# A latent-attention preparation on Trainium2: rotation, root, tables and constants put in another order and on another engine

## The chip, the cores and the metric

The kernel runs on one core of one Trainium2 chip. The metric is device time in microseconds, the median of several executions. The engines of a core are TensorE (PE in the profile, its weight loads PEld), VectorE (DVE), ScalarE (ACT), GpSimd (POOL) and SyncE (SP), whose queue issues nearly all transfers here. Each engine takes its instructions in the order in which they were compiled, and waits on semaphores where an input or a buffer is not there yet.

## The reference, cut to what matters

One layer of a decoder with three attention branches over 2048 tokens of width 1024: `x + W_out(concat(A, B, C) * silu(z))`. Branch A, multi-head latent attention with 8 heads, is the one whose preparation is changed:

```
q  = (rms_norm(cq, q_norm_g) @ w_uq).reshape(b, s, 8, 96)
kv = (rms_norm(ckv, kv_norm_g) @ w_ukv).reshape(b, s, 8, 128)
k_nope, v = kv[..., :64], kv[..., 64:]
k = concatenate([k_nope, broadcast(k_rope)], -1)
q = rms_norm(q, qn_g);  k = rms_norm(k, kn_g)
q = concatenate([q[..., :64], rope(q[..., 64:], pos)], -1)      # the same for k
o = softmax(causal(q k^T / sqrt(96))) v
```

Branch B is differential attention (4 heads with two softmax maps each, an RMS norm on its output), branch C attention into 256 memory tokens.

## The kernel before

**Stages.** The program is one list of steps, each for one block of 512 tokens (b = 0 to 3) and one group of heads: four steps `m` (memory), eight `d` (differential), sixteen `a` (latent: groups g = 0 to 3 of two heads). A step is prepared (`prep_m`, `prep_d`, `prep_a`), then its attention maps run (`Map`: scores into the PSUM tile `st`, an Exp on ScalarE at L506, the low part `plo` of the result on VectorE at L507, the products with V into `pv`), then a post stage (`post_d`, `post_y`) gates and transposes its output. Other work (projections, gates, output projection) is fed in between as generators.

**Order.** A loop at the end of `hybrid_block` picks at each turn the preparation, the fill or the map whose due position comes first, and each piece gets a priority. Nothing of this is the final order: the tile framework (`TileContext(nc, schedule_with_timeline_sim=True)`) then gives every engine its order with a timeline simulated at compile time, taking at each moment what is ready and has the best priority. So an instruction can be placed far ahead of where its line stands, when its inputs and its buffer are free, and every changed line can move others.

**One latent preparation, `prep_a`.** TensorE projects four tiles of 128 tokens; ScalarE copies queries `q` (L844) and keys `kn` (L845) out of PSUM and makes V. ScalarE squares the keys (L853) and the queries (L855); VectorE sums the squares (L854, L857). GpSimd makes the step's rotary tables times the norm weights (`rope_tabs`, four multiplies, L332 to L335, into the tile `rtab`, which has one buffer), adds the shared key part's squares (L861), and takes the inverse root in `rstd_of`: an addition of eps at L97 and a power of -0.5 at L101. With the root, GpSimd scales the shared rotated key (L866); VectorE scales the keys' 64 own columns (L871), multiplies them with the norm weights `g_n` (L872), and scales the queries (L874). GpSimd has rotated the queries' last 32 columns in place (`rope_in_place`, five instructions, L354 to L358, the first two by the sine into a scratch that is part of the squares' tile). The rotation doesn't need the root, and the root doesn't need the rotation; L874 needs both.

For each of the two heads the result is then split into a high and a low f16 part in a stack tile (`ks` for K, `qs` for Q; all stacks of the kernel share six buffers): ScalarE copies the high part (L880, L886), VectorE subtracts for the low part (L881, L887), GpSimd fills columns 96 to 127 with a constant (memsets at L879 and L885, 128 x 256 f16 each), and SP issues a transposing transfer into `kT` or `qB`. A stack buffer becomes free when its transposing transfer has read it. `est_block` then computes rough score maxima (L398, tiles `pe`, `ec`, `er`) and writes them into column 96 of `qs`.

**`post_d`.** The differential output's norm: eight squares on ScalarE (L596), `rstd_of` (L97, L101), then one more GpSimd multiply by 1/64 (L599) ahead of VectorE's L602.

The functions that the diff touches, and what calls them:

Of the kernel before, what the change touches and what calls it, by code (L numbers as in the profile page):

```python
# [15 lines left out]
AF = mybir.ActivationFunctionType  # L16
ALU = mybir.AluOpType
# [8 lines left out]
EPS = 1e-6  # L26
NEG = -1.0e30
WS = 64.0
MS = 32.0
# [11 lines left out]
def hybrid_block(ctx: ExitStack, tc: tile.TileContext, x, mem, positions, norm_g, w_in, mla_q_norm_g,  # L41
# [46 lines left out]
    gx = gain_cols(norm_g, NK, "gx", WS)  # L88
    gm = gain_cols(mem_norm_g, NK, "gm", WS, G)

    def rstd_of(ss, shape, name, tag="rstd"):
        r = sm.tile([P, 32 if tag == "rstd" else 8], F32, tag=tag, name=name)
        n = int(np.prod(shape))
        rv = r[:, 0:n]
        if len(shape) == 2:
            rv = rv.rearrange("p (a b) -> p a b", b=shape[1])
        G.tensor_scalar(rv, ss, EPS, None, ALU.add)  # L97
        m = mhalf
        if len(shape) == 2:
            m = m.unsqueeze(2)  # L100
        G.tensor_tensor(rv, rv, m.broadcast_to([P] + list(shape)), ALU.pow)  # L101
        return rv
# [96 lines left out]
    def new_qkv(name):  # L199
        return wk.tile([P, 4, 256], F32, tag="qkv", name=name, bufs=2)  # L200
# [103 lines left out]
    g_q = gain_row(mla_qn_g, 96, "g_q")  # L304
# [21 lines left out]
    def rope_tabs(b, g, name):  # L326

        tb = wk.tile([P, 2, 4, 32], F32, tag="rtab", name=f"rt_{name}", bufs=1)
        c = cos_t[:, 4 * b:4 * b + 4, :]
        s = sin_t[:, 4 * b:4 * b + 4, :]  # L330
        g1, g2 = _bc(g[:, 0:16], 1, 4), _bc(g[:, 16:32], 1, 4)
        G.tensor_tensor(tb[:, 0, :, 0:16], c, g1, ALU.mult)  # L332
        G.tensor_tensor(tb[:, 0, :, 16:32], c, g2, ALU.mult)
        G.tensor_tensor(tb[:, 1, :, 0:16], s, g2, ALU.mult)
        G.tensor_tensor(tb[:, 1, :, 16:32], s, g1, ALU.mult)  # L335
        return tb
# [12 lines left out]
    def rope_in_place(q, tb, nh, eng, tmp):  # L349

        tmp = tmp.rearrange("p (t h d) -> p t h d", t=4, d=32)
        C = _bc(tb[:, 0], 2, nh)
        Sn = _bc(tb[:, 1], 2, nh)
        eng.tensor_tensor(tmp[..., 0:16], q[..., 16:32], Sn[..., 0:16], ALU.mult)  # L354
        eng.tensor_tensor(tmp[..., 16:32], q[..., 0:16], Sn[..., 16:32], ALU.mult)
        eng.tensor_tensor(q, q, C, ALU.mult)
        eng.tensor_tensor(q[..., 0:16], q[..., 0:16], tmp[..., 0:16], ALU.subtract)
        eng.tensor_tensor(q[..., 16:32], q[..., 16:32], tmp[..., 16:32], ALU.add)  # L358
# [231 lines left out]
    def post_d(st, y):  # L590
        y8 = y.rearrange("p t h d -> p (t h) d")
        ss = sm.tile([P, 8], F32, tag="yss", name=f"yss_{st.name}")
        ys = new_ys(4 + st.g, st.b)
        sink = ys[:, 0].rearrange("p t k -> p (t k)")
        for i in range(8):
            A.activation(sink[:, 64 * i:64 * i + 64], y8[:, i, :], AF.Square, scale=1.0 / 8.0, accum_out=ss[:, i:i + 1])  # L596
        yield 1.0
        r = rstd_of(ss[:, 0:8], [8], f"yr_{st.name}", "rstd_y")
        G.tensor_scalar(r, r, 1.0 / WS, None, ALU.mult)  # L599
        yield 1.0  # L600
        yield 1.0
        V.tensor_tensor(y8, y8, _bc(r, 2, 64), ALU.mult)  # L602
        yield 1.0
        yf = y.rearrange("p t h d -> p t (h d)")
        V.tensor_tensor(yf, yf, st.z, ALU.mult)
        yield 1.0
        yield from finish(st, yf, 4 + st.g, ys)
# [216 lines left out]

    def prep_a(st):
        g, b, nm = st.g, st.b, st.name
        q = new_qkv(f"qkv_{nm}")[:, :, 0:192].rearrange("p t (h d) -> p t h d", d=96)
        knt = tmp4(f"kn_{nm}")
        kn = knt[:, 0:768].rearrange("p (t h d) -> p t h d", t=4, d=96)
        vt = new_v(b, nm)  # L830
        G.memset(vt[:, :, :, 64:65], WS)
        for t in range(4):
            ps = ps_p.tile([P, 512], F32, tag="pp", name="pp")
            q0, k0 = 192 * g, 256 * g
            first = True
            for c in range(2):
                for hx, hw in ((0, 0), (0, 1), (1, 0)):
                    T.matmul(ps[:, 0:192], lhsT=lat_q[b][:, t, hx, c, :], rhs=wuq[c][:, hw, q0:q0 + 192], start=first,
                             stop=False, skip_group_check=True)
                    first = False  # L840
            for i, (hx, hw) in enumerate(((0, 0), (0, 1), (1, 0))):
                T.matmul(ps[:, 192:448], lhsT=lat_kv[b // 2][:, b % 2, t, hx, :], rhs=wukv[0][:, hw, k0:k0 + 256],
                         start=False, stop=(i == 2), skip_group_check=True)
            A.activation(q[:, t], ps[:, 0:192].rearrange("p (h d) -> p h d", d=96), AF.Copy, scale=1.0 / WS)  # L844
            A.activation(kn[:, t, :, 0:64], ps[:, 192:320].rearrange("p (h d) -> p h d", d=64), AF.Copy, scale=1.0 / WS)  # L845
            put_v(vt[:, t], ps[:, 320:448].rearrange("p (h d) -> p h d", d=64))
            yield 1.6
        sqt = tmp4(f"sqq_{nm}")
        sq = sqt[:, 0:768].rearrange("p (t h d) -> p t h d", t=4, d=96)
        ss = sm.tile([P, 2, 8], F32, tag="ssa", name=f"ss_{nm}")  # L850
        for i, m in enumerate((sqt, knt)):
            sk = m[:, 768:1024].rearrange("p (t h d) -> p t h d", t=2, d=64)
            A.activation(sk, kn[:, 2 * i:2 * i + 2, :, 0:64], AF.Square, scale=1.0 / math.sqrt(96))  # L853
            V.reduce_sum(ss[:, 1, 4 * i:4 * i + 4], sk.rearrange("p t h d -> p (t h) d"), axis=AX.X)  # L854
        A.activation(sq, q, AF.Square, scale=1.0 / math.sqrt(96))  # L855
        yield 1.0
        V.reduce_sum(ss[:, 0, :], sq.rearrange("p t h d -> p (t h) d"), axis=AX.X)  # L857
        tb = rope_tabs(b, g_q[:, 64:96], nm)
        yield 1.0
        s4 = ss[:, 1, :].rearrange("p (t h) -> p t h", h=2)  # L860
        G.tensor_tensor(s4, s4, _bc(ss_kr[b], 2, 2), ALU.add)  # L861
        r = rstd_of(ss.rearrange("p a b -> p (a b)"), [16], f"r_{nm}")
        rq = r[:, 0:8].rearrange("p (t h) -> p t h", h=2)
        rk = r[:, 8:16].rearrange("p (t h) -> p t h", h=2)
        yield 1.0
        G.tensor_tensor(kn[..., 64:96], _bc(krot[b], 2, 2), _bc(rk, 3, 32), ALU.mult)  # L866
        rope_in_place(q[..., 64:96], tb, 2, G, sqt[:, 768:1024])
        yield 1.0
        yield 1.0
        yield 1.0  # L870
        V.tensor_tensor(kn[..., 0:64], kn[..., 0:64], _bc(rk, 3, 64), ALU.mult)  # L871
        V.tensor_tensor(kn[..., 0:64], kn[..., 0:64], _bc(_bc(g_n, 1, 2), 1, 4), ALU.mult)  # L872
        yield 1.0
        V.tensor_tensor(q, q, _bc(rq, 3, 96), ALU.mult)  # L874
        kT = bigt([P, 2, 4, 2, P], f"kT_{nm}") if b in AB else kvp.tile([P, 2, 4, 2, P], F16, tag="kT", name=f"kT_{nm}")
        st.qs, st.qB = [], []
        for h in range(2):
            ks = stack([P, 4, 2, P], f"ks{h}_{nm}")
            G.memset(ks[:, :, :, 96:128], MS)  # L879
            A.activation(ks[:, :, 0, 0:96], kn[:, :, h], AF.Copy)  # L880
            V.tensor_tensor(ks[:, :, 1, 0:96], kn[:, :, h], ks[:, :, 0, 0:96], ALU.subtract)  # L881
            SP.dma_start_transpose(kT[:, h].rearrange("p t l k -> p (t l) k"), ks.rearrange("p t l d -> p (t l d)"))
            yield 1.0
            qs = stack([P, 2, 4, P], f"qs{h}_{nm}")
            G.memset(qs[:, :, :, 96:128], 0.0)  # L885
            A.activation(qs[:, 0, :, 0:96], q[:, :, h], AF.Copy)  # L886
            V.tensor_tensor(qs[:, 1, :, 0:96], q[:, :, h], qs[:, 0, :, 0:96], ALU.subtract)  # L887
            st.qs.append(qs)
            st.qB.append(new_qb([P, 2, 4, P], f"qB{h}_{nm}"))
            SP.dma_start_transpose(st.qB[h].rearrange("p l t k -> p (l t) k"), qs.rearrange("p l t d -> p (l t d)"))  # L890
            yield 1.0
        st.kTs = st.prev.kTs + [kT] if b else [kT]
        st.Vs = st.prev.Vs + [vt] if b else [vt]
        yield 1.0
        yield 1.0
        for h in range(2):
            yield from est_block(st, h, 1, lambda m: st.qs[h][:, 0, :, 96], lambda m, t: st.qB[h][0:96, 0, t, :],
                                 lambda m, c, n: st.kTs[c][0:96, h, 0:n, 0, :])
            SP.dma_start_transpose(st.qB[h][:, 0], st.qs[h][:, 0].rearrange("p t d -> p (t d)"))
            ready.add((nm, h))  # L900
            yield 1.0
# [361 lines left out]
```

## Time and profile before

| | us |
|---|---|
| runs shown: median (lowest to highest) of three | 1380.5 (1380.03 to 1385.78) |
| the profiled execution, its own time | 1382.39 |
| its span, first to last instruction | 1380.7 |
| mean granted TensorE clock | 0.983 |
| TensorE busy, with weight loads apart | 1297.6 |
| VectorE busy | 1113.6 |
| ScalarE busy | 902.8 |
| GpSimd busy | 353.4 |

A row of waits or idle time says who waited and which instruction released it; `L` numbers are lines of the kernel. A matmul counts as busy while it is in the pipeline, so a busy TensorE is not always one at its peak, and the granted clock is a share of full speed.

### The profile page before, as it was taken

To read this page: it belongs to the slowest core of one execution; us is meant where nothing else is said; L and a number is where in the kernel's file an instruction comes from. 1 tells how busy PE (TensorE), PEld (TensorE's weight loads), DVE (VectorE), ACT (ScalarE), POOL (GpSimd) and SP (SyncE) were. 2 spreads that over 40 slices of the span, in tenths; PEclk is the share of its full clock that TensorE was granted. 3 is DMA by queue.
4 is the path that set the end of the run, shared out by engine and by line. 5 is a ranking of instruction groups with operands and counts; after the bars stand their busy time and mean duration, and the time that the engine had idled before them with its cause. 6 is when DMAs were issued, how large, how long until landed. Compare 5 with 4: busy or idle time off the path is not lost.

```text
span 1380.7 us, 35076 instructions
## 1 busy us (share of the span) xinstructions
PE 1297.6 (94%) x13616; PEld 834.4 (60%) x13616; DVE 1113.6 (81%) x2649; ACT 902.8 (65%) x2163; POOL 353.4 (26%) x549
## 2 busy tenths in 40 slices
PE   5988999999999999999999999999998988999998
PEld 2443556667677767767776656656665665655554
DVE  4657888879888867888998888988898888986745
ACT  6656544687877646786986567766766777774521
POOL 2322132403052233113212233232353333200000
PEclk9999999999999999999999999999999999999999
DMA  7998844323113322447345275446535443275452
GB/s 229 199 210 179 183 109 98 59 59 87 42 24 71 78 38 56 78 115 190 118 98 142 55 147 146 104 93 157 117 70 123 124 96 64 43 149 157 138 192 69
DMA packets 294263, 155.53 MB, mean 113 GB/s; under 512 B 239952, under 2 KB 272848, under 8 KB 294096
## 3 DMA queue, kind: packets, MB, share of 16 engines
q1 hardware_dynamic: 294064, 153.29, 47.1%
q8 instruction: 106, 1.74, 0.5%
q14 instruction: 61, 0.50, 0.1%
q0 software_dynamic: 32, 0.00, 0.0%
HBM read 61.75 MB, written 34.34 MB: 70 GB/s over the span
## 4 chain that ended last, share of the span: by engine, by line
PE 53%; DVE 14%; DMA 10%; POOL 9%; ACT 8%; issue 5%; SPq 1%; ACTq 0%; POOLq 0%; DVEq 0%
PE pp L187 6%; PE pp L188 6%; PE pp L189 6%; PE pe L398 5%; DVE plo L507 4%; PE pv L518 3%; PE pv L516 3%; PE pv L536 3%; PE st L572 3%; PE pp L957 3%; PE pp L958 3%; PE pp L959 3%; POOL r_a L101 2%; PE st L916 2%; PE st L917 2%
## 5 line engine op out<-in xcount | busy, mean ns | idle before, releaser
L506 ACT ACTIVATE p<-st 128x512 f32<-128x512 f32 (+3 forms) x672 | 356.1, 550 | 178.0 <-PE st L918 72.2
L507 DVE TENSOR_TENSOR plo<-p 128x512 f16<-128x512 f32 (+3 forms) x672 | 405.6, 615 | 61.9 <-ACT p L506 58.7
L407 ACT ACTIVATE ec<-pe 128x512 bf16<-128x512 f32 (+3 forms) x384 | 197.6, 536 | 34.1 <-PE pe L400 15.2
L516 PEld LDWEIGHTS <-p 128*128 128x128 bf16 x2304 | 187.0, 99 | 49.3 <-issue 5.1
L518 PEld LDWEIGHTS <-p 128*128 128x128 bf16 x2304 | 173.8, 98 | 41.5 <-issue 4.4
L408 DVE TENSOR_TENSOR er<-er,ec 128x512 bf16<-128x512 bf16 (+3 forms) x384 | 141.0, 377 | 29.9 <-ACT ec L407 15.1
L404 ACT ACTIVATE er<-pe 128x512 bf16<-128x512 f32 x192 | 110.2, 606 | 44.2 <-DVE mx_d L413 14.1
L536 PEld LDWEIGHTS <-plo 128*128 128x128 f16 x2304 | 123.6, 98 | 24.0 <-DVE plo L507 8.6
L916 PE MATMUL st<-qB_a,kT_a 97*128 97x512 f16 (+1 forms) x320 | 112.6, 352 | 19.2 <-ACT p L506 14.3
L189 PEld LDWEIGHTS <-ht_x 128*128 128x128 f16 x896 | 87.8, 98 | 54.8 <-ACT ht_x L137 5.1
L188 PEld LDWEIGHTS <-ht_x 128*128 128x128 f16 x896 | 87.8, 98 | 50.2 <-issue 6.4
L572 PE MATMUL st<-qB_d,kT_d 97*128 97x512 f16 (+1 forms) x320 | 112.2, 355 | 6.0 <-DMA qB_d<-s_d 2.9
L516 PE MATMUL pv<-V_d,p 128*128 128x65 f16 x1088 | 116.4, 194 | 0.8 <-DVE y_d L579 0.8
L187 PEld LDWEIGHTS <-ht_x 128*128 128x128 f16 x896 | 87.8, 98 | 46.6 <-issue 2.9
L518 PE MATMUL pv<-V_d,p 128*128 128x64 f16 x1088 | 115.9, 196 | 0.0
L516 PE MATMUL pv<-V_a,p 128*128 128x65 f16 x1088 | 113.9, 194 | 0.4 <-DVE y_a L923 0.4
L518 PE MATMUL pv<-V_a,p 128*128 128x64 f16 x1088 | 113.2, 196 | 0.0
L917 PE MATMUL st<-qB_a,kT_a 96*128 96x512 f16 (+1 forms) x320 | 112.3, 351 | 0.0
L398 PE MATMUL pe<-kT_d,qB_d 96*128 96x512 f16 (+2 forms) x320 | 106.4, 351 | 6.0 <-ACT ec L407 3.5
L918 PE MATMUL st<-qB_a,kT_a 96*128 96x512 f16 (+1 forms) x320 | 111.6, 349 | 0.0
L398 PE MATMUL pe<-kT_a,qB_a 96*128 96x512 f16 (+2 forms) x320 | 102.4, 353 | 6.6 <-DMA qB_a<-qs_a 3.1
L189 PE MATMUL pp<-w_d,ht_x 128*128 128x512 f16 x256 | 97.0, 379 | 0.0
(294 smaller groups left out, 3356.1 us busy)
## 6 DMA issues: line engine op xcount, KB each, us to landing
xt_x<-in_x_dram SPq DMA_DIRECT2D x16, 512.0 KB, 4.6
xr<-in_x_dram SPq DMA_DIRECT2D x16, 512.0 KB, 3.7
part<-xr SPq DMA_DIRECT2D x16, 512.0 KB, 3.1
ysc<-yt SPq DMA_DIRECT2D x31, 256.0 KB, 2.1
yl<-ysc SPq DMA_DIRECT2D x15, 512.0 KB, 4.4
zsc<-zc SPq DMA_DIRECT2D x48, 128.0 KB, 2.2
xa<-part SPq DMA_DIRECT2D x12, 512.0 KB, 3.6
out_dram<-xa SPq DMA_DIRECT2D x12, 512.0 KB, 3.3
```

Source lines behind the costliest of these rows:

```text
L187: T.matmul(ps[:, :n], lhsT=ht[:, 0, k], rhs=wt[:, 0, :n], start=(k == 0), stop=False)
L188: T.matmul(ps[:, :n], lhsT=ht[:, 0, k], rhs=wt[:, 1, :n], start=False, stop=False)
L189: T.matmul(ps[:, :n], lhsT=ht[:, 1, k], rhs=wt[:, 0, :n], start=False, stop=(k == NK - 1))
L398: T.matmul(ps[:, 0:n], lhsT=lhs(m, t), rhs=rhs(m, c, n // P), start=True, stop=c < b)
L407: A.activation(ec[:, 0:n], ps[:, 0:n], AF.Copy)
L408: V.tensor_tensor(er[:, t % 2, 0:n], er[:, t % 2, 0:n], ec[:, 0:n], ALU.max)
L506: A.activation(p32[:, :n], ps[:, :n], AF.Exp, scale=self.scale)
L507: V.tensor_tensor(plo[:, :n], p32[:, :n], phi[:, :n], ALU.subtract)
L516: T.matmul(pvv[:, t, 0:65], lhsT=phi[:, c], rhs=vt[:, 0:65], start=(j == 0 and t == 0), stop=False, skip_group_check=True)
L518: T.matmul(pvv[:, t, 0:64], lhsT=phi[:, c], rhs=vt[:, 65:129], start=False, stop=False, skip_group_check=True)
L536: last["pv"] = T.matmul(pvv[:, t, 0:65], lhsT=plo[:, c], rhs=vt[:, 0:65], start=False, stop=(j == self.njt - 1), skip_group_check=True)
L572: T.matmul(ps[:, :n], lhsT=st.kTs[j // 4][0:97, h, j % 4, m % 2, :], rhs=st.qB[h][0:97, t0:4, m % 2, :], start=True, stop=not diag)
```

## The change

Four things change in `prep_a`, one in `post_d`. (1) `rope_tabs` is called at the top of `prep_a`. (2) `rope_in_place` is issued ahead of L861 and the root, in place of behind L866. (3) The multiply by the norm weights `g_n` is issued ahead of the root, on keys that aren't scaled yet. (4) The four memsets of a step go from GpSimd to VectorE, each behind the subtract into the same tile (`tc.issue_after` puts an instruction behind a given one on its engine). (5) `post_d` folds the factor 1/64 into the squares' scale and eps, by a new argument of `rstd_of`, and drops L599.

```
-    def rstd_of(ss, shape, name, tag="rstd"):
+    def rstd_of(ss, shape, name, tag="rstd", eps=EPS):
...
-        G.tensor_scalar(rv, ss, EPS, None, ALU.add)
+        G.tensor_scalar(rv, ss, eps, None, ALU.add)
...
     def post_d(st, y):
...
-            A.activation(sink[:, 64 * i:64 * i + 64], y8[:, i, :], AF.Square, scale=1.0 / 8.0, accum_out=ss[:, i:i + 1])
-        yield 1.0
-        r = rstd_of(ss[:, 0:8], [8], f"yr_{st.name}", "rstd_y")
-        G.tensor_scalar(r, r, 1.0 / WS, None, ALU.mult)
+            A.activation(sink[:, 64 * i:64 * i + 64], y8[:, i, :], AF.Square, scale=WS / 8.0, accum_out=ss[:, i:i + 1])
+        yield 1.0
+        r = rstd_of(ss[:, 0:8], [8], f"yr_{st.name}", "rstd_y", EPS * WS * WS)
...
     def prep_a(st):
         g, b, nm = st.g, st.b, st.name
+        tb = rope_tabs(b, g_q[:, 64:96], nm)
...
         V.reduce_sum(ss[:, 0, :], sq.rearrange("p t h d -> p (t h) d"), axis=AX.X)
-        tb = rope_tabs(b, g_q[:, 64:96], nm)
-        yield 1.0
+        V.tensor_tensor(kn[..., 0:64], kn[..., 0:64], _bc(_bc(g_n, 1, 2), 1, 4), ALU.mult)
+        yield 1.0
+        rope_in_place(q[..., 64:96], tb, 2, G, sqt[:, 768:1024])
         s4 = ss[:, 1, :].rearrange("p (t h) -> p t h", h=2)
         G.tensor_tensor(s4, s4, _bc(ss_kr[b], 2, 2), ALU.add)
         r = rstd_of(ss.rearrange("p a b -> p (a b)"), [16], f"r_{nm}")
...
         G.tensor_tensor(kn[..., 64:96], _bc(krot[b], 2, 2), _bc(rk, 3, 32), ALU.mult)
-        rope_in_place(q[..., 64:96], tb, 2, G, sqt[:, 768:1024])
...
         V.tensor_tensor(kn[..., 0:64], kn[..., 0:64], _bc(rk, 3, 64), ALU.mult)
-        V.tensor_tensor(kn[..., 0:64], kn[..., 0:64], _bc(_bc(g_n, 1, 2), 1, 4), ALU.mult)
...
         for h in range(2):
             ks = stack([P, 4, 2, P], f"ks{h}_{nm}")
-            G.memset(ks[:, :, :, 96:128], MS)
             A.activation(ks[:, :, 0, 0:96], kn[:, :, h], AF.Copy)
-            V.tensor_tensor(ks[:, :, 1, 0:96], kn[:, :, h], ks[:, :, 0, 0:96], ALU.subtract)
+            lo = V.tensor_tensor(ks[:, :, 1, 0:96], kn[:, :, h], ks[:, :, 0, 0:96], ALU.subtract)
+            with tc.issue_after(lo.ins):
+                V.memset(ks[:, :, :, 96:128], MS)
...
             qs = stack([P, 2, 4, P], f"qs{h}_{nm}")
-            G.memset(qs[:, :, :, 96:128], 0.0)
             A.activation(qs[:, 0, :, 0:96], q[:, :, h], AF.Copy)
-            V.tensor_tensor(qs[:, 1, :, 0:96], q[:, :, h], qs[:, 0, :, 0:96], ALU.subtract)
+            lo = V.tensor_tensor(qs[:, 1, :, 0:96], q[:, :, h], qs[:, 0, :, 0:96], ALU.subtract)
+            with tc.issue_after(lo.ins):
+                V.memset(qs[:, :, :, 96:128], 0.0)
```

## Rows read from the trace of the kernel before

**Rows 1.** The page's busy time: us (share of the span) xinstructions.
```profile
PE 1297.6 (94%) x13616; PEld 834.4 (60%) x13616; DVE 1113.6 (81%) x2649; ACT 902.8 (65%) x2163; POOL 353.4 (26%) x549
```

**Rows 2.** Busy time by stretch; behind the engines: granted clock, DMA share, GB/s.
```profile
680.00:1250.00 570.00, 534.46 (x6126) 352.65 (x6124) 499.75 (x1191) 401.41 (x983) 175.76 (x285) 0.97 0.48 108
...
700.00:750.00 50.00, 48.92 (x583) 33.86 (x581) 47.94 (x118) 38.55 (x96) 13.04 (x23) 1.00 0.49 125
```

**Rows 3.** Waits: engine and line, what released it, total us, times, longest.
```profile
POOL qs_a L885 <- DMA kT_a<-ks_a: 59.3, 12, 11.3
...
ACT qs_a L886 <- DVE qkv_a L874: 17.7, 7, 6.7
...
DVE kn_a L871 <- POOL r_a L101: 16.2, 10, 4.3
...
PE st L916 <- ACT p L506: 14.3, 14, 4.3
```

**Rows 4.** Timeline of 1046 to 1062 us: start, us, engine, line [idle before].
```profile
1046.41 0.92 ACT L855 ACTIVATE sqq_a<-qkv_a 128x768 f32<-128x768 f32 x1
...
1048.77 0.31 POOL L885 MEMSET qs_a<- 128x256 f16 x1 [0.45 <-DMA kT_a<-ks_a]
1049.05 2.20 POOL L354 TENSOR_TENSOR sqq_a<-qkv_a,rt_a 128x128 f32<-128x128 f32 x1
...
1053.44 0.32 POOL L332 TENSOR_TENSOR rt_a<-cos_t,g_q 128x64 f32<-128x64 f32 x1
...
1055.70 2.92 POOL L101 TENSOR_TENSOR r_a<-r_a,mhalf 128x16 f32<-128x16 f32 x1
...
1061.78 0.37 PE L916 MATMUL st<-qB_a,kT_a 97*128 97x256 f16 x1 [4.34 <-ACT p L506]
```

**Rows 5.** Timeline of 1006 to 1021 us.
```profile
1006.22 0.88 ACT L855 ACTIVATE sqq_a<-qkv_a 128x768 f32<-128x768 f32 x1
...
1008.66 0.31 POOL L879 MEMSET ks_a<- 128x256 f16 x1 [1.56 <-DMA qB_a<-qs_a]
...
1020.24 0.38 PE L398 MATMUL pe<-kT_a,qB_a 96*128 96x512 f16 x1 [1.94 <-ACT ec L407]
```

**Rows 6.** Timeline of 1101 to 1111 us.
```profile
1101.73 0.86 ACT L855 ACTIVATE sqq_a<-qkv_a 128x768 f32<-128x768 f32 x1
...
1104.20 0.31 POOL L885 MEMSET qs_a<- 128x256 f16 x1 [4.76 <-DVE ss_a L857]
...
1105.82 0.96 POOL L354 TENSOR_TENSOR sqq_a<-qkv_a,rt_a 128x128 f32<-128x128 f32 x1
...
1109.77 0.28 ACT L845 ACTIVATE kn_a<-pp 128x128 f32<-128x128 f32 x1 [2.70 <-POOL qkv_a L358]
...
1110.92 0.48 PE L916 MATMUL st<-qB_a,kT_a 97*128 97x384 f16 x1 [3.49 <-ACT p L506]
```

**Rows 7.** Busy time in three stretches of 10 us, columns as in Rows 2.
```profile
1020.00:1030.00 10.00, 9.75 (x95) 6.66 (x95) 10.00 (x24) 7.83 (x22) 3.92 (x10) 0.83 0.28 54
1060.00:1070.00 10.00, 8.22 (x84) 6.46 (x84) 9.76 (x21) 8.06 (x23) 0.39 (x2) 0.83 0.62 145
1110.00:1120.00 10.00, 9.08 (x109) 7.24 (x109) 8.52 (x18) 6.64 (x19) 5.24 (x6) 0.69 0.26 57
```

**Rows 8.** The chain that ended last, by engine, share of the span.
```profile
PE 53%; DVE 14%; DMA 10%; POOL 9%; ACT 8%; issue 5%; SPq 1%; ACTq 0%; POOLq 0%; DVEq 0%
```

**Rows 9.** Groups by line and form: xcount | busy us, mean ns | idle before.
```profile
L507 DVE TENSOR_TENSOR plo<-p 128x256 f16<-128x256 f32 x64 | 27.1, 423 | 6.8 <-ACT p L506 6.6
...
L408 DVE TENSOR_TENSOR er<-er,ec 128x256 bf16<-128x256 bf16 x48 | 14.6, 303 | 2.9 <-ACT ec L407 1.4 <-ACT er L404 1.0
...
L872 DVE TENSOR_TENSOR kn_a<-kn_a,g_n 128x512 f32<-128x512 f32 x16 | 11.0, 685 | 0.0
...
L421 DVE TENSOR_SCALAR qs_a<-mx_a 128x4 f16<-128x4 f32 x32 | 5.7, 177 | 0.4
...
L599 POOL TENSOR_SCALAR yr_d<-yr_d 128x8 f32<-128x8 f32 x8 | 2.0, 252 | 0.7
```

## The prediction

> **What bounds the kernel now.** I read the page's busy shares first, then busy time by stretch, then the list of waits, then the timeline around single waits. TensorE is busy 1297.6 of 1380.7 us [rows 1], so whatever the change does on other engines, it can give back only what TensorE idles or runs at the lower clock: 83.1 us idle in the span. `prep_a`, which holds most of the diff, runs 16 times, nearly all of it in 680 to 1250 us. There TensorE is busy 534.46 of 570 us at a granted clock of 0.97 [rows 2]: 35.5 us idle, and 0.03 x 570 = 17 us of full-speed time lost to the clock. These 52 us are all that the main part of the change can win. In the same stretch VectorE is busy 499.75 of 570 us, 88%: it is the second bound, and it is given more work here.
>
> The waits tell where TensorE's idle time comes from [rows 3]. TensorE waits 14.3 us for the score buffer `st`, which ScalarE's Exp (L506) frees; ScalarE stands 17.7 us before L886 until VectorE has scaled the queries (L874); VectorE stands 16.2 us before L871 until GpSimd has the root (L101). Each engine takes its instructions in order, so a late root stops VectorE, then ScalarE, then TensorE. And GpSimd stands a further 59.3 us before L885, a memset, until an earlier transposing transfer has freed the stack buffer it fills. Most of that is harmless, GpSimd being busy only 353.4 us. It costs where the next step's rotation is queued behind it.
>
> Three places show that, and they hold the largest of TensorE's waits that go back to this chain:
> - 1057 us [rows 4]: ScalarE has the squares (L855) at 1046.41 + 0.92 = 1047.33, but the L885 memset waits for a transfer until 1048.77. Only then do the rotation (L354, 1049.05), the next step's tables (L332, 1053.44) and the root (L101, 1055.70, 2.92 us) follow. TensorE idles 4.34 us.
> - 1018 us [rows 5]: the L879 memset stands in the middle of the rotation until 1008.66 + 0.31; the squares were there at 1007.10. TensorE idles 1.94 us.
> - 1107 us [rows 6]: the memset at 1104.20 comes ahead of L354 at 1105.82, though the squares were there at 1102.59. The rotation's end (L358) is what ScalarE's L845 waits for (2.70 us, its buffer is the rotation's scratch), and TensorE idles 3.49 us.
> Behind each, the granted clock falls: 0.83, 0.83 and 0.69 in the 10 us after or around it [rows 7], a mixture of the two levels 2.4 and 1.2 GHz. That costs 1.7 + 1.7 + 3.1 = 6.5 us.
>
> **Constants by VectorE: GpSimd's side.** 64 memsets (two tiles, two heads, 16 steps) leave GpSimd's queue, and with them their waits. In the first place the rotation's multiplies by the sine need only the queries, and the third multiply could start with the squares at 1047.33; it started after L354's end at 1051.25, 3.9 us later. In the second it went on at 1008.97 and could have at 1007.10, 1.9 us. In the third L354 could start with the end of the squares at 1102.59, if VectorE's sums free its scratch by then, in place of 1105.82: 3.2 us. TensorE's gaps are each a little larger than these, so they shrink by the whole: 3.9 + 1.9 + 3.2 = 9.0 us. Bounds: nothing (another late instruction takes the memset's place) to 9.8 us, the three gaps. I take 9.0, because in each place the rows lead from the memset to the gap without another wait. Of the clock's 6.5 us I take half, 3.2; bounds 0 and 6.5. Next late after the memset is ScalarE's copy into the same stack buffer, which waits for the same transfer as before; nothing there gets worse.
>
> **Constants by VectorE: VectorE's side.** No VectorE memset is in this trace. Bounds from rows [rows 9]: above the smallest f16 write of VectorE, 0.177 us (L421), and below a two-operand f32 instruction over 256 columns, 0.423 (L507); I take 0.303 (L408, 256 16-bit columns), which it is nearest to. 64 x 0.303 = 19.4 us more VectorE work. The memset waits for nothing new: the subtract ahead of it has already written the tile. Behind it on VectorE are the low parts `plo`; on SP the transposing transfer now starts a memset later. What VectorE time costs at the end I price by its share of the chain that ended last, 14%, and the transfers by theirs, 10% [rows 8]: 19.4 x 0.24 = 4.6 us. Bounds: 64 x 0.177 x 0.14 = 1.6 us, and, with VectorE never free, 64 x 0.423 x 0.88 = 23.8 us. I take 4.6, as VectorE has 12% free time on average.
> The Trainium skill (VectorE: DVE Perf Modes, section "Zero memsets can be issued as uint32 (trn2)") says that a memset takes one cycle per element whatever the type; at the 0.96 GHz of its table my estimate from it is 256 / 0.96 = 267 ns, 17.1 us in all, which would make the term 4.1 in place of 4.6. No run here shows it yet; it speaks against any hope that the moved memsets are nearly free.
>
> **Norm weights ahead of the root.** L872 (16 x 0.685 = 11.0 us [rows 9]) leaves the stretch between root and K's copies for VectorE's wait before the root. At 14% that is a gain of 1.5 us; bounds nothing, and 10 x 0.685 = 6.9 us if it fills each of the ten waits. I take 1.5.
> The Trainium skill (SBUF — State Buffer, section "Who interferes with whom") says that a VectorE instruction with two SBUF inputs contends with a GpSimd one that reads SBUF, and L872, such a one, moves beside the rotation. The trace has L354 at 0.96 us [rows 6] and at 2.20 [rows 4], which may be this; my estimate is 11.0 us at GpSimd's 9%, a loss of 1.0 us. I leave it out, since VectorE runs other instructions with two operands there anyway.
>
> **Tables first, rotation first.** In 13 of the 16 steps the trace already has the rotation ahead of the root, and between them the tables of the *next* step: from L332 to the root 1053.44 to 1055.70, 2.3 us with two small instructions of the root's own among them [rows 4]. The order is the scheduler's: the table tile has one buffer, which becomes free when L356 has read it, and GpSimd is given whatever is ready. The diff moves where the tables are issued, not when the buffer becomes free, so I expect them to stay in front of the root: 0. Bound: 13 x 2.3 = 30 us off GpSimd's path to the root, of which no more can count than TensorE still idles. In the last three steps the root now waits for two more rotation instructions (under 0.96 us each, the length of L354 in [rows 6]), while the queries are ready sooner: 0.
>
> **The eps folded in (`post_d`).** Eight instructions (L599, 0.252 us [rows 9]) go: 2.0 us x 9% = 0.2.
>
> **Sum.** -9.0 - 3.2 + 4.6 - 1.5 - 0.2 = -9.3 us. The profiled execution took 1382.39 us, 1.7 around its span and 1.9 above the median of the runs, 1380.5: 1373.1 for it, 1371.2 against the median. About 0.5%, 6.9 us, is what a measurement of this kernel can tell from no change.
>
> **Rivals.**
> 1. *The tables do leave the front of the root.* Then the root comes up to another 2.3 us sooner in most steps. The rest of TensorE's wait for L506, 14.3 - 4.3 - 3.5 = 6.5 us, goes, and the other half of the clock: -9.3 - 6.5 - 3.3 = -19.1, 1361.4 us. For: they are issued first. Against: the single buffer.
> 2. *The memset's waits were one of several.* All engine orders are made anew; waits for transfers (TensorE's on `qB_a`, say) open where the memsets' close. Half of the 9.0 comes, nothing of the clock, and the 4.6 is paid: -4.5 + 4.6, 1380.6 us. For: the memset's hold decides in only three of 16 steps.
> 3. *VectorE becomes the bound (slower).* In 700 to 750 us VectorE is busy 47.94 of 50 us [rows 2], 2.1 free. 16 steps in 570 us are 1.4 in 50, with four memsets each: 1.7 us. Where a stretch has less free time than that, memsets push back `plo`, and with it Exp's buffers. If most stretches are so: 19.4 x 0.88 = 17.1 lost, and half of the 13.9 gained: +10.1, 1390.6 us. For: several places near 95%. Against: the 88% mean.
>
> **How the numbers follow.** Forecast 0.36, rival 1 0.14, rival 2 0.30, rival 3 0.20. Faster 0.50, same 0.30, slower 0.20. Predicted 1371.2. The range reaches down to rival 1 and up to the middle between rivals 2 and 3: 1361 to 1386. The forecast's own range, with the clock's 3.2 either way and the VectorE term between 1.6 and 7, is 1365 to 1377.
>
> **What would show it.** Right: no memset on GpSimd in `prep_a`; VectorE's wait for L101 well under 16.2 us and ScalarE's for L874 under 17.7; VectorE memset rows near 0.3 us; TensorE's idle time in 680 to 1250 under 30 us. Wrong: VectorE busy 95% there with `st` waits unchanged (rival 3), or the three gaps closed and others open (rival 2), or tables seen behind the root (rival 1).

## The result, and the profile after

The changed kernel takes 1372.15 us in the median (1371.2 to 1375.3), the kernel before beside it on the same chip 1381.99: a ratio of 0.993, interval [0.9912, 0.9947]. The forecast was 1371.2, 9.3 us below the 1380.5 of the three runs that it knew; against all five runs of the kernel before, the change measured 9.8. The time came as forecast; the experiments below speak against the forecast's reason.

The profiled execution after took 1372.15 us with a span of 1370.3 and a mean granted clock of 0.989. Busy time on its page, against [rows 1]:

```profile
PE 1293.0 (94%) x13616; PEld 829.5 (61%) x13616; DVE 1123.1 (82%) x2713; ACT 903.9 (66%) x2163; POOL 333.9 (24%) x477
```

VectorE has 64 instructions and 9.5 us more, GpSimd 72 instructions (64 memsets and eight of L599) and 19.5 us less. TensorE's 13616 instructions took 4.6 us less, and the span fell by 10.4 us, so TensorE idles 77.3 us in place of 83.1. Busy time by stretch, columns as in [rows 2]:

```profile
680.00:1250.00 570.00, 538.39 (x6181) 350.44 (x6179) 509.90 (x1255) 403.92 (x983) 155.95 (x211) 0.98 0.49 112
```

TensorE idles 31.6 us here against 35.5, VectorE is at 89% against 88, and the clock is at 0.98 against 0.97. The waits, columns as in [rows 3]:

```profile
ACT ks_a L878 <- POOL kn_a L867: 13.2, 10, 3.0
...
PE st L917 <- ACT p L506: 8.7, 13, 2.5
...
DVE kn_a L871 <- POOL r_a L101: 7.0, 11, 1.2
```

VectorE's wait for the root fell from 16.2 to 7.0 us and TensorE's for the score buffer from 14.3 to 8.7. ScalarE's wait before the queries' copy for VectorE's scaling (17.7 in [rows 3]) is 1.4 us in all; a new one stands at its copy of the keys, 13.2 us for GpSimd's product of the shared key part with the root (L867). The new VectorE memsets, by line and form:

```profile
L881 DVE MEMSET ks_a<- 128x256 f16 x32 | 8.7, 272 | 0.1
L888 DVE MEMSET qs_a<- 128x128 uint32 x32 | 5.3, 165 | 0.0
```

VectorE's busy time rose by 9.5 us and not by these 14.0, since the rows of neighbouring instructions overlap by some 0.07 us (416.45 + 0.41 against 416.79 in the rows below).

And one step's GpSimd instructions in the timeline:

```profile
721.96 0.50 POOL L358 TENSOR_TENSOR qkv_a<-qkv_a,sqq_a 128x128 f32<-128x128 f32 x1
722.42 0.63 POOL L332 TENSOR_TENSOR rt_a<-cos_t,g_q 128x64 f32<-128x64 f32 x1
...
724.59 0.48 POOL L97 TENSOR_SCALAR r_a<-ss_a 128x16 f32<-128x16 f32 x1
725.15 2.92 POOL L101 TENSOR_TENSOR r_a<-r_a,mhalf 128x16 f32<-128x16 f32 x1
```

The next step's tables (L332) still stand between the rotation's end (L358) and the root (L101), as the prediction had it.

**Where the time is gained.** VectorE takes a reciprocal (L526) at the end of each of the 80 attention maps, so the ends, counted in order of time, can be compared between kernels (in the latent stage, where the orders differ, the nth end need not be the same map's). Each kernel has one profiled execution. Up to the 28th end the two stay within 1.3 us of each other; between the 28th and the 29th the changed kernel gains 3.2 us. This is the group of that line in 400 to 440 us, first and last start being the ends of these two maps; before:

```profile
L526 DVE RECIPROCAL rl<-pv x2: 167/172/178, 406.4 to 434.7; 128x4 f32<-128x4 f32 x2
```

and after:

```profile
L526 DVE RECIPROCAL rl<-pv x2: 168/170/171, 406.0 to 431.1; 128x4 f32<-128x4 f32 x2
```

Busy time between these two ends, columns as in [rows 2], before and after:

```profile
406.40:434.70 28.30, 22.46 (x303) 16.99 (x301) 23.91 (x68) 20.34 (x53) 11.88 (x15) 0.88 0.29 63
406.00:431.10 25.10, 20.56 (x310) 16.38 (x308) 24.45 (x70) 20.00 (x54) 7.97 (x16) 0.93 0.33 71
```

VectorE idles 4.4 us before and 0.7 after. TensorE idles 1.3 us less and is busy 1.9 us less, at a granted clock of 0.93 in place of 0.88.

At the 42nd end (661.0 us before) the changed kernel is 3.9 us ahead, at the 80th 10.6. So 3.2 us come from one place in the differential stage, where only `post_d` was changed, 0.4 us were there before it, and 6.7 us come from the latent stage behind 660 us. The first of these, in the timeline of VectorE and GpSimd before:

```profile
413.04 1.35 DVE L408 TENSOR_TENSOR er<-er,ec 128x512 bf16<-128x512 bf16 x4
413.08 4.10 POOL L97 TENSOR_SCALAR yr_d<-yss_d 128x8 f32<-128x8 f32 x1 [0.77 <-ACT ys L596]
414.31 0.68 DVE L507 TENSOR_TENSOR plo<-p 128x512 f16<-128x512 f32 x1
414.92 0.41 DVE L412 TENSOR_TENSOR er<-er 128x512 bf16<-128x512 bf16 x1
415.25 0.68 DVE L507 TENSOR_TENSOR plo<-p 128x512 f16<-128x512 f32 x1
415.85 0.68 DVE L745 TENSOR_TENSOR lk<-kl,lk 128x512 f16<-128x512 f32 x1
416.45 0.41 DVE L466 TENSOR_TENSOR s_d<-qkv_d,s_d 128x256 f16<-128x256 f32 x1
416.79 0.28 DVE L412 TENSOR_TENSOR er<-er 128x256 bf16<-128x256 bf16 x1
417.23 0.56 POOL L462 MEMSET s_d<- 128x256 f16 x2
417.75 1.67 POOL L101 TENSOR_TENSOR yr_d<-yr_d,mhalf 128x8 f32<-128x8 f32 x1
419.51 0.25 POOL L599 TENSOR_SCALAR yr_d<-yr_d 128x8 f32<-128x8 f32 x1
419.80 0.69 DVE L602 TENSOR_TENSOR y_d<-y_d,yr_d 128x512 f32<-128x512 f32 x1 [2.73 <-POOL yr_d L599]
```

and after:

```profile
414.02 0.68 DVE L408 TENSOR_TENSOR er<-er,ec 128x512 bf16<-128x512 bf16 x2
414.63 0.41 DVE L466 TENSOR_TENSOR s_d<-qkv_d,s_d 128x256 f16<-128x256 f32 x1
414.66 0.48 POOL L97 TENSOR_SCALAR yr_d<-yss_d 128x8 f32<-128x8 f32 x1 [2.98 <-ACT ys L596]
415.08 0.42 DVE L408 TENSOR_TENSOR er<-er,ec 128x512 bf16<-128x512 bf16 x1
415.23 1.81 POOL L101 TENSOR_TENSOR yr_d<-yr_d,mhalf 128x8 f32<-128x8 f32 x1
...
417.11 0.68 DVE L601 TENSOR_TENSOR y_d<-y_d,yr_d 128x512 f32<-128x512 f32 x1
```

The addition of eps (L97) on 8 columns takes 4.10 us before and 0.48 after. Before, VectorE runs without a pause from 413.04 to 416.79 + 0.28 = 417.07 us, and L97 ends 0.11 us behind that, at 417.18; then VectorE, its queue at L602, waits 2.73 us for GpSimd, which has two memsets (L462), the power and L599 still to do. After, VectorE has a pause of 0.04 us at 414.63 + 0.41 = 415.04, L97 ends 0.10 us behind its start, the two memsets had been done earlier (411.12), and L601 waits for nothing. In all seven kernels with the new `post_d` this L97 takes 0.48 to 0.49 us, in all seven without it 4.09 to 4.10. The Trainium skill (SBUF — State Buffer, "Who interferes with whom") says that a VectorE instruction with two SBUF inputs and a GpSimd one that reads SBUF contend for one port pair, an exclusive lock; these rows agree with it, a 0.48 us instruction lasting as long as VectorE's unbroken run.

The edit doesn't remove such holds. The changed kernel has one itself at the fourth `post_d`, where the kernel before has 0.42 us:

```profile
503.82 2.36 POOL L97 TENSOR_SCALAR yr_d<-yss_d 128x8 f32<-128x8 f32 x1 [1.44 <-ACT ys L596]
```

VectorE waits 2.05 us for that root, the 33rd end comes 1.6 us later, and at the 34th the lead is back. So it is in all seven kernels whose L97 takes 2.35 to 2.36 us there; in the seven where it takes 0.42 to 0.55 the 33rd end does not shift. The two groups cut across the parts of the change. So a hold can also cost nothing in the end.

### The profile page after: what moved, and what is told of

The parts are those of the page before. It is cut to its first block, busy times and chain, and to the rows that moved or that the text cites. A ratio compares the mean times of both kernels' runs of the same rounds, so it can differ in the third digit from the quotient of the medians.

```text
span 1370.3 us, 35041 instructions
## 1 busy us (share of the span) xinstructions
PE 1293.0 (94%) x13616; PEld 829.5 (61%) x13616; DVE 1123.1 (82%) x2713; ACT 903.9 (66%) x2163; POOL 333.9 (24%) x477
## 4 chain that ended last, share of the span: by engine, by line
PE 56%; DVE 13%; POOL 9%; ACT 8%; DMA 8%; issue 4%; SPq 1%; ACTq 0%; DVEq 0%; POOLq 0%
PE pp L189 6%; PE pp L187 6%; PE pp L188 6%; PE pe L398 5%; DVE plo L507 4%; PE pv L518 3%; PE pv L516 3%; PE pv L536 3%; PE st L572 3%; PE pp L958 3%; PE pp L959 3%; PE pp L960 3%; PE st L917 3%; PE st L918 2%; PE st L919 2%
## 5 line engine op out<-in xcount | busy, mean ns | idle before, releaser
L506 ACT ACTIVATE p<-st 128x512 f32<-128x512 f32 (+3 forms) x672 | 356.2, 551 | 167.2 <-PE st L919 65.8
L407 ACT ACTIVATE ec<-pe 128x512 bf16<-128x512 f32 (+3 forms) x384 | 197.2, 536 | 39.2 <-PE pe L400 17.1
L408 DVE TENSOR_TENSOR er<-er,ec 128x512 bf16<-128x512 bf16 (+3 forms) x384 | 141.5, 378 | 29.9 <-ACT ec L407 15.2
L398 PE MATMUL pe<-kT_d,qB_d 96*128 96x512 f16 (+2 forms) x320 | 106.2, 348 | 6.8 <-ACT ec L407 3.6
L398 PE MATMUL pe<-kT_a,qB_a 96*128 96x512 f16 (+2 forms) x320 | 100.0, 349 | 7.7 <-DMA qB_a<-qs_a 4.6
```

The source lines that it names most:

```text
L398: T.matmul(ps[:, 0:n], lhsT=lhs(m, t), rhs=rhs(m, c, n // P), start=True, stop=c < b)
L407: A.activation(ec[:, 0:n], ps[:, 0:n], AF.Copy)
L506: A.activation(p32[:, :n], ps[:, :n], AF.Exp, scale=self.scale)
```

## The experiments

The parts are numbered as in the change: 1 tables first, 2 rotation ahead of the root, 3 norm weights ahead of it, 4 memsets by VectorE, 5 `post_d`. Each ratio is to the kernel before, run on the same chip.

**The memsets alone (part 4).** The kernel before with

```
-            G.memset(ks[:, :, :, 96:128], MS)
...
+            lo = V.tensor_tensor(...)                  # the subtract into the same tile
+            with tc.issue_after(lo.ins):
+                V.memset(ks[:, :, :, 96:128], MS)      # and the same for qs
```

> The kernel before with the fourth part of the change alone: the four memsets of a latent step on VectorE, each behind its subtract. Theory (the memsets' waits in GpSimd's queue held the rotation back): by the sum, -9.0 - 3.2 + 4.6 = -7.6 us of the -9.3, so a ratio of 0.993 to 0.996, with the wait of L871 for the root down from 16.2 us to 10 or less, and no gap of TensorE over 3 us in 1000 to 1120 us. Rival (the gain came from the norm weights' place and the new order, the memsets only cost VectorE time): 1.000 to 1.004, with VectorE's wait for the root near 16 us.

Measured 0.9992 [0.9977, 1.0007]. The term that carried the forecast is worth nothing that can be told by itself. A wait of TensorE for ScalarE in 680 to 1250 us in the kernel before, beside those of [rows 3]:

```profile
PE pe L398 <- ACT ec L407: 2.8, 3, 1.9
```

and with the memsets moved:

```profile
DVE kn_a L871 <- POOL r_a L101: 12.2, 9, 3.5
...
PE st L918 <- ACT p L506: 9.8, 14, 1.8
PE pe L398 <- ACT ec L407: 8.0, 9, 1.8
```

The prediction's three gaps are closed: in 1000 to 1120 us no wait of TensorE is over 0.9 us. TensorE's wait for the score buffer is 4.5 us shorter, and its wait for the rough scores' buffer (L398, which ScalarE's L407 frees) 5.2 us longer. The root is waited for less (12.2 us in place of 16.2), though not the 10 or less that the theory asked for.

**All but the memsets (parts 1, 2, 3, 5).** The changed kernel with `G.memset` put back.

> The changed kernel with the four memsets of a latent step back on GpSimd, ahead of the copies as before: parts one, two, three and five alone. Theory: little is left, -1.5 - 0.2 of the -9.3, a ratio of 0.998 to 1.001 against the kernel before, with TensorE gaps over 3 us behind memset holds again. Rival (norm weights and order): 0.992 to 0.995.

Measured 0.9923 [0.99, 0.9945], median 1372.75: the whole gain, with the memsets on GpSimd. Its waits, columns as in [rows 3]:

```profile
POOL ks_a L878 <- DMA qB_a<-qs_a: 75.0, 8, 14.8
...
DVE kn_a L871 <- POOL r_a L101: 22.8, 12, 5.1
...
PE st L915 <- ACT p L506: 12.6, 11, 3.5
```

GpSimd again stands before its memsets for transfers, TensorE has a wait of 3.5 us for the score buffer again, and VectorE waits longer for the root than in the kernel before (22.8 against 16.2), in a kernel as fast as the changed one. So neither the memsets' waits nor the total lateness of the root decides the time here.

**The norm weights alone (part 3).** The kernel before with L872 ahead of the root:

```
         V.reduce_sum(ss[:, 0, :], sq.rearrange("p t h d -> p (t h) d"), axis=AX.X)
+        V.tensor_tensor(kn[..., 0:64], kn[..., 0:64], _bc(_bc(g_n, 1, 2), 1, 4), ALU.mult)
...
-        V.tensor_tensor(kn[..., 0:64], kn[..., 0:64], _bc(_bc(g_n, 1, 2), 1, 4), ALU.mult)
```

> The kernel before with the third part alone: the multiply by the norm weights issued ahead of the root. Theory: -1.5 us, a ratio of 0.997 to 1.001; VectorE's wait for the root falls by up to 0.69 us in each of ten places, to about 10 us, yet GpSimd's root stays late. Rival (the norm weights carry the gain): 0.994 or less.

Measured 1.0088 [1.0062, 1.0115], 12 us slower, where the prediction had a gain of 1.5. VectorE does the same work in it.

**The tables where they don't wait for the one buffer.** The changed kernel with

```
+        qt = new_qkv(f"qkv_{nm}")
-        tb = rope_tabs(b, g_q[:, 64:96], nm)
+        tb = rope_tabs(b, g_q[:, 64:96], nm, qt[:, :, 192:256].rearrange("p t (i d) -> p i t d", i=2))
...
```

so that the tables lie in unused columns of the step's own query tile.

> The changed kernel with a latent step's tables in columns 192 to 255 of its own query tile, which has two buffers, in place of the one table buffer: the next step's tables no longer become ready in the middle of the rotation and should stand behind the root. If the tables in front of the root still cost (the first rival of the prediction): up to 2.3 us sooner roots in most steps, another 5 to 10 us off the changed kernel, 1362 to 1367 us, a ratio of 0.986 to 0.990 against the kernel before. If the root was no longer what TensorE waits for: the ratio of the changed kernel, 0.992 to 0.995.

Measured 0.9987 [0.997, 1.0005]. The tables do leave the front of the root, in all 16 steps. One step's rows from the rotation's end (L358) to the root (L101):

```profile
722.85 0.91 POOL L358 TENSOR_TENSOR qkv_a<-qkv_a,sqq_a 128x128 f32<-128x128 f32 x1
723.73 0.19 POOL L863 TENSOR_TENSOR ss_a<-ss_a,sskr 128x8 f32<-128x8 f32 x1
724.01 0.48 POOL L97 TENSOR_SCALAR r_a<-ss_a 128x16 f32<-128x16 f32 x1
724.58 3.18 POOL L101 TENSOR_TENSOR r_a<-r_a,mhalf 128x16 f32<-128x16 f32 x1
```

The root starts 0.82 us behind L358's end (724.58 - 723.76) in place of 2.69 (725.15 - 722.46), VectorE's wait for it is 8.2 us in all against 7.0, and the time is that of the kernel before. What rival 1 priced at 10 us below the forecast is not there in this order.

**`post_d` alone (part 5).** The kernel before with the folded scale and eps:

```
-            A.activation(sink[...], y8[:, i, :], AF.Square, scale=1.0 / 8.0, accum_out=ss[:, i:i + 1])
+            A.activation(sink[...], y8[:, i, :], AF.Square, scale=WS / 8.0, accum_out=ss[:, i:i + 1])
...
-        r = rstd_of(ss[:, 0:8], [8], f"yr_{st.name}", "rstd_y")
-        G.tensor_scalar(r, r, 1.0 / WS, None, ALU.mult)
+        r = rstd_of(ss[:, 0:8], [8], f"yr_{st.name}", "rstd_y", EPS * WS * WS)
```

> The kernel before with the fifth part alone: the factor folded into the squares' scale and eps of post_d, one GpSimd instruction less. The prediction priced it at 0.2 us. Theory from the traces so far: it gives about 3 us in one place, near 415 to 430 us, where VectorE waited 2.7 us for the dropped instruction and TensorE and the clock behind it; the runs that have this part are 3 to 4 us ahead from there on. Ratio 0.997 to 0.999. Rival (the 3 us are the new order's, not this part's): no step near 415 to 430 us.

Measured 0.9978 [0.996, 0.9996]. The two map ends:

```profile
L526 DVE RECIPROCAL rl<-pv x2: 168/169/170, 408.2 to 433.3; 128x4 f32<-128x4 f32 x2
```

25.1 us apart, as in the changed kernel; 28.3 before.

**Tables and rotation alone (parts 1, 2).** The kernel before with the two lines moved.

> The kernel before with parts one and two alone: tables at the top of the step, rotation issued ahead of the root. The prediction priced them at 0: ratio 0.998 to 1.002. Rival (after the memsets failed to carry the gain, these parts do): 0.993 to 0.996.

Measured 1.0003 [0.9987, 1.0019].

**Nothing changed but the order of issue.** The kernel before with one existing memset issued later in the same function:

```
-        G.memset(vt[:, :, :, 64:65], WS)
...                                   (behind the projections and copies)
+        G.memset(vt[:, :, :, 64:65], WS)
```

> A control: the kernel before with only the small memset of V's column 64 (GpSimd, 0.13 us, 16 of them) issued behind the four projections in place of ahead of them. No work, wait or engine changes, only the priorities and with them the order that is made. If an order made anew is worth nothing in itself: ratio 0.998 to 1.002. Rival (each new order is a draw worth several us either way): outside of that, up to 1 per cent.

Measured 1.0048 [1.0028, 1.0068]: 6.6 us for an edit that adds and removes no instruction. Since every engine's order is arranged anew for each program, one moved line moves others, and this is what that alone can do.

**Tables, rotation and norm weights (parts 1 to 3).**

> Parts one, two and three together, memsets on GpSimd and post_d as before. All parts but the memsets gave 0.9923, weights alone 1.0088. If the fifth part is worth 3 us and the rest comes from the weights being ahead of the root together with the rotation: ratio 0.993 to 0.996. Rival (no part has a price of its own, the order decides): anything between 0.993 and 1.009 that the parts' single results don't add up to.

Measured 1.0053 [1.0033, 1.0073]: slower, though with `post_d` added (all but the memsets, above) it is the fastest kernel of all, level with the changed one.

**The same control on the changed kernel.** The memset edit of the first control, applied to the changed kernel.

> The changed kernel with the same null edit that made the kernel before 0.5% slower (V's column memset is issued behind the projections): no work is added or taken away, only the instruction order is made anew. If the 0.993 of the changed kernel belongs to what the change does (the post_d rotation that gives 4 us between 406 and 435 us, and shorter waits around the root): 0.990 to 0.996, and the 28th to 29th map end keep their 4 us. If some 5 us of it belong to one order that came out well: 0.997 to 1.003, with the 4 us at 406 to 435 us kept and the gain between 680 and 1230 us gone.

Measured 1.0012 [0.9996, 1.0027], median 1385.07 against 1382.78: the gain is gone, and the expectation of a lasting gain in the latent stage with it. (The changed kernel itself was not run again beside this one; the kernel before is at 1381.75 to 1382.78 beside the experiments and was at 1381.99 beside the changed kernel.) The two map ends:

```profile
L526 DVE RECIPROCAL rl<-pv x2: 168/169/170, 407.2 to 432.3; 128x4 f32<-128x4 f32 x2
```

The gain at 406 us is kept (25.1 us). What is lost is behind it. Its waits:

```profile
ACT ks_a L878 <- POOL kn_a L867: 23.0, 11, 3.1
DVE kn_a L871 <- POOL r_a L101: 15.9, 13, 2.0
PE st L917 <- ACT p L506: 15.0, 19, 2.4
```

and its stretch, columns as in [rows 2]:

```profile
680.00:1250.00 570.00, 531.04 (x6098) 349.01 (x6097) 504.28 (x1252) 399.50 (x980) 159.07 (x212) 0.98 0.46 108
```

VectorE's wait for the root and TensorE's for the score buffer are back at what [rows 3] shows (16.2 and 14.3), and TensorE idles 39.0 us, more than the 35.5 of before, with every part of the change in place (in a fixed stretch of time, in which it got through 28 matmuls fewer). At the 44th end (701.6 us before) this kernel is 1.3 us ahead of the one before, at the 62nd (1037.2 us) 7.0 behind; the changed one is 11.1 ahead there.

**A second control on the changed kernel.** The two neighbouring ScalarE copies of queries and keys in the other order:

```
-            A.activation(q[:, t], ps[:, 0:192]...)
             A.activation(kn[:, t, :, 0:64], ...)
+            A.activation(q[:, t], ps[:, 0:192]...)
```

> The changed kernel with two ScalarE copies of the preparation issued in the other order: a second edit that adds and removes no work. If the gain belongs to what the change does: 0.990 to 0.996. If it is one order among many: anywhere from 0.990 to 1.005, with only the 4 us at 406 to 435 us kept.

Measured 1.0008 [0.999, 1.0026]. TensorE's wait for the score buffer is 14.2 us, VectorE's for the root 11.8.

**All but `post_d` (parts 1 to 4).**

> The change without its post_d rotation; tables and query rotation ahead of the root, norm weights ahead of it and constants by VectorE stay. Theory (post_d is worth some 4 us by itself, the rest of the change some 6 us in the attention with preparation): 0.995 to 0.997, and the 4 us between 406 and 435 us are lost. Rival (the parts in the preparation give nothing lasting; the order decides): 1.000 to 1.006, as tables, rotation and weights gave without the memsets (1.0053).

Measured 1.0103 [1.0081, 1.0124], the slowest kernel of all; the theory's 0.995 to 0.997 is missed by far, and the rival's range too. The map ends show the loss at `post_d`:

```profile
L526 DVE RECIPROCAL rl<-pv x2: 168/170/172, 408.5 to 438.4; 128x4 f32<-128x4 f32 x2
```

29.9 us apart, 4.8 more than the 25.1 with it. Another 7.9 us are lost behind the 42nd end.

**The shared key part's product by VectorE.** The changed kernel with

```
-        G.tensor_tensor(kn[..., 64:96], _bc(krot[b], 2, 2), _bc(rk, 3, 32), ALU.mult)
+        V.tensor_tensor(kn[..., 64:96], _bc(krot[b], 2, 2), _bc(rk, 3, 32), ALU.mult)
```

> The changed kernel with the product of the shared key part and the root on VectorE in place of GpSimd. ScalarE's copy of that part waits 13.2 us in all for GpSimd in the changed kernel; that wait should be gone, and VectorE has some 16 more small instructions. If ScalarE's wait for GpSimd behind the root sets the end: 0.988 to 0.991. If it does not, or VectorE, busy 89% of this stretch, pays for it: 0.993 to 1.003.

Measured 1.0003 [0.9991, 1.0014]. Of ScalarE's and VectorE's waits:

```profile
ACT ks_a L878 <- DVE kn_a L871: 14.2, 11, 2.4
DVE kn_a L867 <- POOL r_a L101: 13.5, 11, 2.8
```

ScalarE's 13.2 us for GpSimd became 14.2 us for VectorE; the wait changed its releaser and hardly its size, and nothing was won. No version beats the changed kernel: all but the memsets is level with it.

## Why the prediction was right in its time and wrong in its reason

**The time.** 1372.15 lies 1 us from the forecast and inside the range. That is luck: 0.993 is one of the times that this change can have. Three programs hold all five parts and the same instructions, in orders that differ: 0.993, 1.0012 and 1.0008. Two hold none of them: 1 and 1.0048. So the order of issue alone moves this kernel by 0.5% (6.6 us) and 0.8% (11 us); the forecast sum was 9.3. Of the prediction's own signs, the waits for the root and for the queries' scaling fell and the memset rows are near 0.3 us, but TensorE's idle time in 680 to 1250 us is 31.6 us and not under 30.

**Memsets off GpSimd's queue, -9.0: the step that failed.** The prediction took the three gaps as the memsets' price "because in each place the rows lead from the memset to the gap without another wait". For the third place that reading was wrong: the memset's row in [rows 6] has its wait ended by VectorE's sum L857 and not by a transfer, so the 3.2 us priced there need not have been the memset's. The three gaps did close; none of their length stands in the changed kernel (TensorE's longest wait for L506 there is 2.5 us, against 4.3), and with the memsets alone TensorE has no wait over 0.9 us in 1000 to 1120 us. But the memsets alone give 0.9992, with another wait of TensorE (L398 for L407) grown by what the first lost, and the change without them gives 0.9923. Three pairs of kernels differ by the memsets alone, and moving them changed the ratio by -0.0008, +0.0007 (0.9923 to 0.993) and +0.0050 (1.0053 to 1.0103), where the term with its clock and its price forecast -0.0055. Each is one order against another, so a small price of the memsets' own can't be ruled out; the 9.0 us are seen in none. A place of the trace told rightly why TensorE idled there, not that the time would stay won when the order is made anew. That is rival 2, which the prediction priced at 1380.6: "All engine orders are made anew; waits for transfers (TensorE's on `qB_a`, say) open where the memsets' close". The memsets alone (1381.67) and the two controls on the changed kernel, at 1383 and 1385 us, are nearest to it, though the wait that grew with the memsets alone was for ScalarE and not for a transfer.

**The clock, -3.2.** 0.97 to 0.98 in the stretch, where 0.01 is 5.7 us: the forecast lies within the rounding. But it is 0.98 in the first changed control too and 0.99 with the memsets alone, and neither has a gain, so a higher granted clock in this stretch did not bring the time.

**VectorE's memsets, +4.6.** The work was over-sized: 8.7 + 5.3 = 14.0 us against 19.4. The filling of the keys' stack takes 0.272 us, the filling of the queries' with zero 0.165, since it was compiled to 128 columns of uint32. The Trainium skill (VectorE: DVE Perf Modes, "Zero memsets can be issued as uint32 (trn2)") has both, one cycle an element whatever the type and zeros at 4 bytes an element: the trace's 0.272 us agrees with the 267 ns that the prediction estimated from it, the zero rows take 0.165 us for half the elements, and the prediction used only the first half of that section. What the 14 us cost at the end can't be told from the scatter; with and without them the two fast kernels are level (0.993, 0.9923). Rival 3, VectorE as the bound, is not borne out: it is at 89%, and the sixteen extra instructions of the last experiment made nothing slower than the controls.

**Norm weights, -1.5.** No gain is seen: alone 1.0088, on top of tables and rotation 1.0053 against 1.0003. Whether they cost something or drew bad orders is open.

**Tables and rotation, 0.** Right in the trace (the tables of the next step stay in front of the root) and in the time (1.0003). Rival 1, the tables gone from there, was made and gave 0.9987 in place of a gain.

**`post_d`, -0.2: right in sign, too small.** The prediction priced the eight removed instructions at their average, 0.25 us each by GpSimd's share of the chain. All seven kernels with the edit need 25.1 us from the 28th to the 29th map end, all seven without it 27.7 to 29.9, 29.1 in the mean, and the rows show why one place decides: the root chain there starts with an L97 stretched to 4.10 us, and VectorE stands behind it. Over the whole time the seven with it have a mean ratio of 0.9977, the seven without (the kernel before among them, at 1) 1.0041. Three pairs differ by `post_d` alone, and it is the faster in each: by 0.0022, by 0.0130 (1.0053 to 0.9923) and by 0.0173 (1.0103 to 0.993). It is the only part with that. Two cautions: in the traces the kernels with the edit have one order of every engine up to 628 us or later, and so have those without, so the gain at 406 us is one pair of orders seen seven times, not seven draws. And the removal of L599 can't be parted there from the order that came with it, since most of the gain is L97's 3.6 us, some 0.6 us is the two memsets (L462) that stood behind it, and only some 0.3 us is L599 and its handing over.

**What stays open.** Some 4 us of the 10 are placed (4.0 between the means of the two groups, 3.2 in the pair shown): `post_d`'s root at 413 us, in every kernel with that edit. The other 6.7 us, in the latent stage, are lost with either control. They are the order's, or need one that both controls broke; the runs can't tell these apart, and no single wait was found that goes with the time over all kernels (VectorE waits 7.0 us for the root in one of the two fastest kernels and 22.8 in the other). The sizes of places are from one execution each: kernels with the same order up to there are 0.3 to 3.9 us ahead at the 42nd end.

## What to carry to other kernels

Where a compiler arranges all engine orders anew, make one or two edits that change nothing but the order, on both kernels, before any gain of that size is given to a part; here they were worth 0.5 to 0.8%. A gap that the trace leads back to one instruction shows why that place idled, and not what the next order will give. What repeats in every kernel with an edit, at the same place, is found by comparing the starts of one marker instruction, not the total times; whether it is the edit's or that of one order which all of them share has to be asked then.

## What the runs showed of the hardware

GpSimd's addition on 128 x 8 f32 took 4.10 us while VectorE ran two-input instructions without a pause, and 0.48 where VectorE paused; its end lay 0.10 to 0.11 us behind the pause's start in both. In the changed kernel one took 2.36 us beside a run that ended at 506.08 us, 0.10 us before it. So the price of a small GpSimd instruction can be the length of VectorE's unbroken run beside it. A VectorE memset of 128 x 256 f16 took 0.272 us, and the zero one of the same bytes, as 128 x 128 uint32, 0.165.
